# A hybrid attention block on one Trainium2 core: the 16 meta rows stand last in h, and k, v and u come in pieces of 384, 384 and 272 columns

## The chip, the cores and the metric

The kernel runs on one core of a Trainium2 chip. Its time is the device time of one execution in microseconds (us); the kernel before has a median of 738.9 us over three runs (737.64 to 739.29). The engines are PE (TensorE matmul), ACT (ScalarE), DVE (VectorE), POOL (GpSimd) and SP (SyncE, which issues most DMAs). Each engine takes its own instructions in a fixed order and waits on semaphores for the others.

## The reference: what is computed

A pre-norm decoder block with two parallel token mixers over 16 meta rows and 1024 tokens (L = 1040 positions, D = 1024):

```
h = rmsnorm(concat([meta, x]), norm_g)
u_pool, z_pool, q, k, v, z_attn, f_logit, g_pool, g_attn = split(h @ w_in)
y_pool = causal_multiscale_pool(u_pool, pool_w, pool_scale) * silu(z_pool)
log_f  = log_sigmoid(f_logit + b_forget)
# 8 heads of 64; logit[t, s] = q_t.k_s / 8 + sum of log_f over (s, t], causal
y_attn = forgetting_attention(q, k, v, log_f) * silu(z_attn)
merged = sigmoid(g_pool) * (y_pool @ w_up_pool) + sigmoid(g_attn) * (y_attn @ w_up_attn)
out    = rmsnorm((x + merged @ w_out), final_norm_g)      # the meta rows are dropped
```

Only k, v, u and the forget gates are needed for the meta rows; q, the other gates and the output are needed for the 1024 tokens alone. Everything is float32; a product is made of three matmuls in the chip's float32r format (high part times high part, and the two mixed terms).

## The kernel before, in words

**Layout.** h is kept transposed (128 rows of the model dimension in each of 8 slices, tokens along the columns) as a high part `hh` and a low part `hl`. In a row of 1088 columns the 1040 positions are the last 1040, so the meta rows are columns 48 to 63 of the row and the first token is column 64. Every projection is `g_proj` (L166): 24 matmuls (8 slices; `hh,whi`, then `hl,whi`, then `hh,wlo`) of 128 weight columns against a piece of the positions, into one PSUM bank `pj` (three banks in turn). q, the gates and z take two pieces of 512; k, v and u take three `PIECES` of 400, 384 and 256 (L29).

**Start (to about 57 us).** Nine tiles of 128 positions are loaded (`norm_load`, L179; the first one takes the 16 meta rows and 112 tokens in two DMAs, the ninth holds the last 16 tokens), normalised (`norm_stat`, `norm_scale`) and transposed on PE (`norm_t`). Between them the q, k and v of head pair 0 are projected in four pieces (0 to 256, 256 to 512, 512 to 768, 768 to 1040, the loop at L452). The ninth tile is transposed in the middle of the third v piece.

**Evictions.** `q_piece` (L244) has ACT write the high part and DVE the low part of q; `k_piece` (L266) does so for k, each head of the pair apart; `v_piece` (L276) has ACT copy the piece to `VT`. `v_blocks(p, b0, b1)` (L284) then transposes blocks b0 to b1 of 128 keys of `VT` on PE, one matmul `pj<-ident,vt` (L287) a block, and ACT (L292) and DVE (L293) evict them to `V`, a high and a low part for each of two heads. In `f_v` (L319) of the later head pairs the blocks follow the pieces: after the piece that begins at 400 come blocks 0 to 2, after the one at 784 blocks 3 to 5, and blocks 6 to 8 come as a step of their own. Key block b holds keys 128b to 128b + 127 (block 8 the last 128), so each group of blocks ends before the piece that has just been computed begins.

**Attention (about 85 to 480 us).** 16 units (4 head pairs, 2 heads, 2 halves of the queries). `qk` (L596) makes two matmuls `ps<-qa,ka` and `ps<-ql,ka` a key block (L608, L609; two `ps` banks in turn), ACT and DVE evict them as `S` (L617, L615); `maxes` finds column maxima on DVE; `soft` subtracts them (DVE L648), exponentiates (ACT L649), and splits the result (`ph` on ACT L652, `pl` on DVE L653); `av` (L663) multiplies with `V` into `po` (L669).

**What sets the order.** PE's order is that of the code (`manual_schedule`). The attention's steps are written out, and between them `F.pull(ns)` takes matmuls of the later projections from generators (`Fill`): the q, k and v of the next head pair, then u, z and the gates, matmul by matmul, until the given time is filled. The order on ACT, DVE, POOL and SP is set by a scheduler when the program is built. `whi<-raw` (L149, ACT) and `wlo` (L151, POOL) split the weights of the next projection. After the attention come the pooling branch, the merge and the output projection, almost without a gap on PE.

## Time and profile before

| | |
|---|---|
| median of 3 runs | 738.9 us (737.64 to 739.29) |
| profiled execution | 738.82 us, its span (first to last instruction) 737.1 us, so 1.7 us lie around the span |
| busy share of the span | PE 98%, DVE 72%, ACT 51%, POOL 42% |
| chain that ended last | PE 88%, DVE 3%, ACT 1%, POOL 1% |
| its largest part | PE pj L163 (the projections) 66% |
| PE idle, 57 to 490 us, as the waits name it | 1.6 us |

How to read it: PE is busy from the start to the end, so the time is, nearly, the sum of the spacings of PE's matmuls and of the few places where PE waits. A matmul's listed duration overlaps the next one; the spacing of two starts is what it costs. What the other engines do matters only where PE waits for it.

### The profile page before, as it was taken

To read this page: it belongs to the slowest core of one execution; us is meant where nothing else is said; L and a number is where in the kernel's file an instruction comes from. 1 tells how busy PE (TensorE), PEld (TensorE's weight loads), DVE (VectorE), ACT (ScalarE), POOL (GpSimd) and SP (SyncE) were. 2 spreads that over 40 slices of the span, in tenths; PEclk is the share of its full clock that TensorE was granted. 3 is DMA by queue.
4 is the path that set the end of the run, shared out by engine and by line. 5 is a ranking of instruction groups with operands and counts; after the bars stand their busy time and mean duration, and the time that the engine had idled before them with its cause. 6 is when DMAs were issued, how large, how long until landed. Compare 5 with 4: busy or idle time off the path is not lost.

```text
span 737.1 us, 10620 instructions
## 1 busy us (share of the span) xinstructions
PE 725.2 (98%) x3686; PEld 624.2 (85%) x3686; DVE 531.6 (72%) x991; ACT 375.8 (51%) x736; POOL 305.9 (42%) x362
## 2 busy tenths in 40 slices
PE   8999999999999999999999999999999999999996
PEld 6997999988889898889888888888887888888885
DVE  4753578859769878788798688687288554887775
ACT  6652555356456645556554564462545422626445
POOL 4322145465435547336436374283349011006243
PEclk9999999999999999999999999999999999999999
DMA  9201123321452355411542346227485357672006
GB/s 302 61 6 53 28 77 88 98 80 30 109 158 51 94 106 107 120 50 42 177 99 84 98 135 152 73 79 240 138 234 187 113 189 269 222 262 72 1 1 229
DMA packets 82312, 86.89 MB, mean 118 GB/s; under 512 B 9889, under 2 KB 61089, under 8 KB 82226
## 3 DMA queue, kind: packets, MB, share of 16 engines
q1 hardware_dynamic: 78272, 77.29, 34.0%
q0 software_dynamic: 2112, 4.19, 3.6%
q10 hardware_dynamic: 1874, 4.72, 1.7%
q8 instruction: 29, 0.48, 0.3%
q14 instruction: 25, 0.20, 0.1%
HBM read 67.12 MB, written 27.46 MB: 128 GB/s over the span
## 4 chain that ended last, share of the span: by engine, by line
PE 88%; DVE 3%; ACT 1%; issue 1%; POOL 1%; POOLq 0%; ACTq 0%; DVEq 0%
PE pj L163 66%; PE pj L1025 8%; PE po L669 5%; PE ps L609 3%; PE ps L608 2%; PE pt L1025 2%; PE pj L494 1%; POOL yl L136 1%; PE pj L287 0%; DVE S L648 0%; ACT whi L149 0%; DVE pl L653 0%; DVE pt L639 0%; DVE S L615 0%; DVE mt L629 0%
## 5 line engine op out<-in xcount | busy, mean ns | idle before, releaser
L151 POOL TENSOR_TENSOR wlo<-raw,whi 128x256 fp32r<-128x256 f32 x148 | 123.5, 879 | 187.2 <-ACT whi L149 95.9
L163 PE MATMUL pj<-hh,whi 128*128 128x512 f32 (+5 forms) x768 | 178.9, 361 | 0.7 <-DVE V L293 0.4
L163 PE MATMUL pj<-hl,whi 128*128 128x512 f32 (+5 forms) x768 | 175.8, 358 | 0.0
L163 PE MATMUL pj<-hh,wlo 128*128 128x512 f32 (+5 forms) x768 | 173.7, 356 | 0.0
L163 PEld LDWEIGHTS pj<-hh,whi 128*128 128x128 f32 x768 | 132.4, 190 | 17.5 <-PE pj L287 0.6
L163 PEld LDWEIGHTS pj<-hh,wlo 128*128 128x128 f32 x768 | 132.2, 188 | 17.1
L163 PEld LDWEIGHTS pj<-hl,whi 128*128 128x128 f32 x768 | 132.2, 189 | 16.6
L653 DVE TENSOR_TENSOR pl<-S,ph 128x512 fp32r<-128x512 f32 (+4 forms) x112 | 88.3, 806 | 14.0 <-ACT ph L652 13.5
L661 POOL TENSOR_TENSOR acc<-acc,S 128x272 f32<-128x272 f32 (+4 forms) x80 | 77.1, 963 | 8.9 <-ACT S L649 3.7
L617 ACT ACTIVATE S<-ps,negc 128x400 f32<-128x400 f32 (+2 forms) x96 | 49.1, 514 | 48.1 <-DVE S L615 40.5
L649 ACT ACTIVATE S<-S 128x512 f32<-128x512 f32 (+4 forms) x112 | 49.7, 478 | 33.6 <-DVE S L648 33.4
L624 DVE TENSOR_TENSOR m<-m,S 128x272 f32<-128x272 f32 (+4 forms) x80 | 40.9, 512 | 23.1 <-ACT S L617 21.3
L652 ACT ACTIVATE ph<-S 128x512 fp32r<-128x512 f32 (+4 forms) x112 | 51.7, 479 | 9.4 <-PE po L669 8.6
L149 ACT ACTIVATE whi<-raw 128x1024 fp32r<-128x1024 f32 x37 | 39.1, 1056 | 33.6 <-PE pj L163 26.0
L648 DVE TENSOR_TENSOR S<-S,pt 128x512 f32<-128x512 f32 (+4 forms) x112 | 51.7, 498 | 0.8
L873 DVE TENSOR_TENSOR rl<-pj,rl 128x512 f32<-128x512 f32 x32 | 22.1, 690 | 31.5 <-PE pj L163 31.5
L669 PE MATMUL po<-pl,V 128*128 128x512 f32 (+4 forms) x112 | 37.5, 335 | 0.1
L609 PE MATMUL ps<-ql,ka 128*128 128x512 f32 (+4 forms) x112 | 37.4, 334 | 0.0
L615 DVE SCALAR_TENSOR_TENSOR S<-ps,negc,mask 128x128 f32<-128x128 f32 (+2 forms) x72 | 23.7, 330 | 18.8 <-PE ps L609 17.9
L608 PE MATMUL ps<-qa,ka 128*128 128x512 f32 (+4 forms) x112 | 35.9, 321 | 1.2 <-ACT S L617 1.2
L325 ACT ACTIVATE st<-pj 128x512 f32<-128x512 f32 x40 | 23.7, 593 | 26.1 <-PE pj L163 18.8
L1025 PE MATMUL pj<-opy 128*128 128x512 f32 (+1 forms) x168 | 36.2, 374 | 0.0
(187 smaller groups left out, 1101.2 us busy)
## 6 DMA issues: line engine op xcount, KB each, us to landing
raw<-in_w_in_dram SPq DMA_DIRECT2D x40, 512.0 KB, 4.0
sp_gp<-st SPq DMA_DIRECT2D x16, 256.0 KB, 2.0
td<-in_w_out_dram POOLq DMA_DIRECT2D x4, 1024.0 KB, 10.2
sp_ga<-st SPq DMA_DIRECT2D x16, 256.0 KB, 2.0
rl<-sp_gp SPq DMA_DIRECT2D x8, 512.0 KB, 5.3
rl<-sp_ga SPq DMA_DIRECT2D x8, 512.0 KB, 4.7
W<-td SPq DMA_DIRECT2D x8, 512.0 KB, 5.3
xr<-in_x_dram SPq DMA_DIRECT2D x8, 512.0 KB, 4.2
```

The lines of the kernel that those rows point to most:

```text
L151: ins = nc.gpsimd.tensor_tensor(lo[:, k:k + 2], raw[:, k:k + 2], r32(hi[:, k:k + 2]), op=ALU.subtract)
L163: nc.tensor.matmul(ps, a, b, start=(i == 0), stop=(i == len(seq) - 1))
L608: nc.tensor.matmul(ps[:kb, c0:], ka[:, k0:k0 + kb], qa[:, q0 + c0:q0 + 512], start=True, stop=False)
L609: nc.tensor.matmul(ps[:kb, c0:], ka[:, k0:k0 + kb], ql[:, q0 + c0:q0 + 512], start=False, stop=True)
L617: nc.scalar.activation(s[:kb, f0:], ps[:kb, f0:], AF.Identity, bias=nb_)
L648: nc.vector.tensor_tensor(s[:kb, c0:], s[:kb, c0:], self.pm[:kb, c0:], op=ALU.subtract)
L649: exps.append(nc.scalar.activation(s[:kb, c0:], s[:kb, c0:], AF.Exp))
L652: nc.scalar.activation(ph[:kb, c0:], s[:kb, c0:], AF.Copy)
L653: dves.append(nc.vector.tensor_tensor(pl[:kb, c0:], s[:kb, c0:], r32(ph[:kb, c0:]), op=ALU.subtract))
L661: accs.append(nc.gpsimd.tensor_tensor(acc[:kb, c0:], acc[:kb, c0:], s[:kb, c0:], op=ALU.add))
L669: nc.tensor.matmul(self.po[:, c0:], v, r[:kb, c0:], start=(b == 0 and i == 0), stop=(b == self.nb - 1 and i == 1))
L1025: nc.tensor.matmul(ps, pick(A_, k, p)[:, i * 128:(i + 1) * 128], pick(B_, k, q)[:, c0:c1], start=start and n == 0, stop=n == 11, skip_grou ...
```

## The change

h holds the 1024 tokens as columns 0 to 1023 and the meta rows as columns 1024 to 1039; a row stays 1088 columns long and the positions are now its first 1040. Tile 0 is loaded by one DMA of 128 tokens, and the ninth tile is the 16 meta rows. The pieces of k, v and u are 384, 384 and 272. Keys, values and u still keep the meta rows in front: `keys_of` maps columns of h to key positions (16 further on, and the meta rows to 0), and where a piece runs past column 1024 its evictions are made in two parts, 256 columns and 16. Key block 0 is now complete only with the last piece, so the block groups of `v_blocks` are 1 to 3, 4 to 6, and 7, 8 and 0; the last group is evicted in two parts for each head.

```
-PIECES = ((0, 400), (400, 784), (784, 1040))
+PIECES = ((0, 384), (384, 768), (768, 1040))
...
-    hh4 = [hp.tile([128, 4, HROW], F32R, name=f"hh{j}")[:, :, HROW - L:] for j in range(2)]
+    hh4 = [hp.tile([128, 4, HROW], F32R, name=f"hh{j}")[:, :, :L] for j in range(2)]
...
-        if i == 0:
-            nc.sync.dma_start(xt[NM:], x2[:128 - NM, :])
-            nc.sync.dma_start(xt[:NM], meta)
-        else:
-            nc.sync.dma_start(xt[:n], x2[c0 - NM:c0 - NM + n, :])
+        nc.sync.dma_start(xt[:n], meta if n < 128 else x2[c0:c0 + n, :])
...
+    def keys_of(t0, t1):
+        r = [(0, min(t1, SEQ) - t0, t0 + NM)]
+        if t1 > SEQ:
+            r.append((SEQ - t0, t1 - t0, 0))
+        return [(slice(a, b), slice(d, d + b - a)) for a, b, d in r]
...
-                nc.scalar.activation(KA[p, e][a, t0:t1], ps[a], AF.Copy)
+                for c, d in keys_of(t0, t1):
+                    nc.scalar.activation(KA[p, e][a, d], ps[a, c], AF.Copy)
...
-        nc.scalar.activation(VT[p][:, t0:t1], ps, AF.Copy)
+        for c, d in keys_of(t0, t1):
+            nc.scalar.activation(VT[p][:, d], ps[:, c], AF.Copy)
...
-    def v_blocks(p, b0, b1):
+    def v_blocks(p, *parts):
         pt = pj.tile([128, 4, 2, 64], F32, name="pj")
-        for b in range(b0, b1):
-            nc.tensor.transpose(pt[:, b - b0], VT[p][:, KS[b]:KS[b] + KB], ident)
-            yield 109.0
...
+        for b0, b1 in parts:
+            for b in range(b0, b1):
+                nc.tensor.transpose(pt[:, n], VT[p][:, KS[b]:KS[b] + KB], ident)
...
             if c0:
-                yield from v_blocks(p, c0 // KB - 3, c0 // KB)
+                yield from v_blocks(p, (c0 // KB - 2, c0 // KB + 1))
...
-            stores.append(nc.sync.dma_start(dt[:, c0:c1], st))
+            for c, d in keys_of(c0, c1):
+                last = nc.sync.dma_start(dt[:, d], st[:, c])
+            stores.append(last)
...
-        todo += [("q", t0, t1), ("k", t0, t1), ("v", t0, t1)]
+        todo += [("q", t0, min(t1, SEQ)), ("k", t0, t1), ("v", t0, t1)]
...
-            run(q_piece(0, wq, max(NM, t0), t1))
+            run(q_piece(0, wq, t0, t1))
...
-            run(v_blocks(0, 2 * (n // 3) - 2, 2 * (n // 3)))
+            run(v_blocks(0, (max(1, 2 * (n // 3) - 2), 2 * (n // 3))))
...
-            F.add(f"v{p}", v_blocks(p, 6, 9), 4 * p - 2, apart=True)
+            F.add(f"v{p}", v_blocks(p, (7, 9), (0, 1)), 4 * p - 2, apart=True)
```

**PE, the second and third v piece of head pair 1.** In the order of the kernel before (`pj<-ident,vt` are the block transposes, `hh_120,wlo` the last matmuls of a piece, `[waits ...]` names the engine that a row waits for):

```order
L163 MATMUL pj<-hh_120,wlo 128x384 x4
L287 MATMUL pj<-ident,vt 128x128 [waits Activation_49]
L287 MATMUL pj<-ident,vt 128x128 x2
L163 MATMUL pj<-hh_119,whi 128x256 x4
L163 MATMUL pj<-hh_120,whi 128x256 x4
L163 MATMUL pj<-hl_121,whi 128x256 x4
L163 MATMUL pj<-hl_122,whi 128x256 x4
L163 MATMUL pj<-hh_119,wlo 128x256 x4
L163 MATMUL pj<-hh_120,wlo 128x256 x4
L287 MATMUL pj<-ident,vt 128x128 [waits Activation_49]
L287 MATMUL pj<-ident,vt 128x128 x2
```

And in that of the changed kernel:

```order
L163 MATMUL pj<-hh_120,wlo 128x384 x4
L293 MATMUL pj<-ident,vt 128x128 [waits Activation_49]
L293 MATMUL pj<-ident,vt 128x128
L293 MATMUL pj<-ident,vt 128x128 [waits Activation_49]
L163 MATMUL pj<-hh_119,whi 128x272 x4
L163 MATMUL pj<-hh_120,whi 128x272 x4
L163 MATMUL pj<-hl_121,whi 128x272 x4
L163 MATMUL pj<-hl_122,whi 128x272 x4
L163 MATMUL pj<-hh_119,wlo 128x272 x4
L163 MATMUL pj<-hh_120,wlo 128x272 x4
L293 MATMUL pj<-ident,vt 128x128 x2
L293 MATMUL pj<-ident,vt 128x128 [waits Activation_49]
```

The pieces and the transposes stand where they stood, but the last of each three transposes now has a wait for ACT of its own: block 3 reads key columns of the piece just before it, and so does block 6.

**ACT, the same place.** `vt<-pj` is the eviction of a v piece, `S<-S` the exponentials, `ph<-S` the high parts, `V<-pj` the evictions of the transposed blocks. Before:

```order
L649 ACTIVATE S<-S 128x512 [waits DVE_49]
L652 ACTIVATE ph<-S 128x512 [waits Activation_49]
L278 ACTIVATE vt<-pj 128x384 [waits PE_49]
L292 ACTIVATE V<-pj 128x3x64 [waits PE_49]
L649 ACTIVATE S<-S 128x512 [waits DVE_49] x2
L292 ACTIVATE V<-pj 128x3x64 [waits DVE_49]
L652 ACTIVATE ph<-S 128x512 [waits Activation_49] x2
L649 ACTIVATE S<-S 128x512 [waits DVE_49]
L278 ACTIVATE vt<-pj 128x256 [waits PE_49]
L292 ACTIVATE V<-pj 128x3x64 [waits PE_49]
L149 ACTIVATE whi<-raw 128x1024 [waits DMAHW3_49]
```

And changed:

```order
L662 ACTIVATE S<-S 128x512 [waits DVE_49]
L665 ACTIVATE ph<-S 128x512 [waits Activation_49]
L282 ACTIVATE vt<-pj 128x384 [waits PE_49]
L662 ACTIVATE S<-S 128x512 [waits DVE_49]
L302 ACTIVATE V<-pj 128x3x64 [waits PE_49]
L665 ACTIVATE ph<-S 128x512 [waits Activation_49]
L662 ACTIVATE S<-S 128x512 [waits DVE_49]
L302 ACTIVATE V<-pj 128x3x64 [waits DVE_49]
L665 ACTIVATE ph<-S 128x512 [waits Activation_49]
L662 ACTIVATE S<-S 128x512 [waits DVE_49]
L149 ACTIVATE whi<-raw 128x1024 [waits DMAHW6_49,PE_49]
L282 ACTIVATE vt<-pj 128x256 [waits PE_49]
```

The second 384-column eviction stands behind the same `S` and `ph` rows as before; the one of 256 columns has moved from ahead of the weight split `whi` to behind it.

**ACT, the first unit of the attention (about 85 to 90 us).** `S<-ps` are the evictions of the scores. Before:

```order
L292 ACTIVATE V<-pj 128x3x64 [waits PE_49]
L271 ACTIVATE ka<-pj 64x384 [waits PE_49]
L292 ACTIVATE V<-pj 128x3x64 [waits DVE_49]
L617 ACTIVATE S<-ps,negc 128x400 [waits DVE_49]
L271 ACTIVATE ka<-pj 64x384 [waits DVE_49]
L617 ACTIVATE S<-ps,negc 128x272 [waits DVE_49]
L149 ACTIVATE whi<-raw 128x1024 [waits PE_49,DMAHW5_49,Activation_49,Pool_49]
L617 ACTIVATE S<-ps,negc 128x144 [waits DVE_49]
L617 ACTIVATE S<-ps,negc 128x16 [waits DVE_49]
```

And changed:

```order
L302 ACTIVATE V<-pj 128x3x64 [waits PE_49]
L273 ACTIVATE ka<-pj 64x384 [waits DVE_49]
L302 ACTIVATE V<-pj 128x64 [waits DVE_49]
L630 ACTIVATE S<-ps,negc 128x400 [waits DVE_49]
L302 ACTIVATE V<-pj 128x3x64 [waits DVE_49]
L630 ACTIVATE S<-ps,negc 128x272 [waits DVE_49]
L302 ACTIVATE V<-pj 128x64 [waits DVE_49]
L630 ACTIVATE S<-ps,negc 128x144 [waits DVE_49]
L149 ACTIVATE whi<-raw 128x1024 [waits PE_49,DMAHW4_49,Activation_49,Pool_49]
```

The weight split `whi` has moved from ahead of the 144-column score eviction to behind it, and the two heads' evictions of `V` have two parts each.

## Rows read from the trace of the kernel before

**Rows 1.** The page: busy time, share of the span and instructions of each engine.

```profile
PE 725.2 (98%) x3686; PEld 624.2 (85%) x3686; DVE 531.6 (72%) x991; ACT 375.8 (51%) x736; POOL 305.9 (42%) x362
```

**Rows 2.** Waits of PE: who waited for whom, us in total, times, longest.

```profile
PE ps L608 <- ACT S L617: 1.2, 2, 0.9
```

**Rows 3.** Timeline, v of pair 1: start, length (us), engine, line, tiles, count [idle before].

```profile
169.67 1.55 PE L163 MATMUL pj<-hh,wlo 128*128 128x384 f32 x8
...
171.06 0.49 PE L287 MATMUL pj<-ident,vt 128*128 128x128 f32 x3
...
171.25 0.63 ACT L649 ACTIVATE S<-S 128x512 f32<-128x512 f32 x1 [1.94 <-DVE S L648]
...
172.44 0.47 ACT L278 ACTIVATE vt<-pj 128x384 f32<-128x384 f32 x1
...
173.30 1.12 PE L163 MATMUL pj<-hh,wlo 128*128 128x256 f32 x8
...
174.26 0.49 PE L287 MATMUL pj<-ident,vt 128*128 128x128 f32 x3
...
175.14 0.47 PE L163 MATMUL pj<-hh,whi 128*128 128x512 f32 x1 [0.39 <-DVE V L293]
...
175.84 0.39 ACT L278 ACTIVATE vt<-pj 128x256 f32<-128x256 f32 x1
...
176.31 1.08 ACT L149 ACTIVATE whi<-raw 128x1024 fp32r<-128x1024 f32 x1
```

**Rows 4.** Timeline, v of pair 2.

```profile
269.92 0.51 PE L287 MATMUL pj<-ident,vt 128*128 128x128 f32 x3
269.94 0.49 ACT L278 ACTIVATE vt<-pj 128x384 f32<-128x384 f32 x1 [2.11 <-PE pj L163]
...
273.36 0.49 PE L287 MATMUL pj<-ident,vt 128*128 128x128 f32 x3
...
274.21 0.37 ACT L278 ACTIVATE vt<-pj 128x256 f32<-128x256 f32 x1
```

**Rows 5.** Timeline, v of pair 3.

```profile
367.51 0.27 PE L287 MATMUL pj<-ident,vt 128*128 128x128 f32 x1
...
367.71 0.49 ACT L278 ACTIVATE vt<-pj 128x384 f32<-128x384 f32 x1 [0.91 <-PE pj L163]
...
372.39 0.49 PE L287 MATMUL pj<-ident,vt 128*128 128x128 f32 x3
...
372.59 0.38 ACT L278 ACTIVATE vt<-pj 128x256 f32<-128x256 f32 x1 [0.20 <-PE pj L163]
```

**Rows 6.** Groups by form: line, engine, tiles, form, count | busy us, mean ns.

```profile
L163 PE MATMUL pj<-hl,whi 128*128 128x400 f32 x80 | 17.9, 348 | 0.0
```

**Rows 7.** Timeline, runs of eight equal matmuls of 400 columns (k of pair 1).

```profile
77.46 1.63 PE L163 MATMUL pj<-hl,whi 128*128 128x400 f32 x8
...
78.93 1.63 PE L163 MATMUL pj<-hh,wlo 128*128 128x400 f32 x8
```

**Rows 8.** Timeline, runs of eight equal matmuls of 272 columns (k of pair 0).

```profile
51.40 1.15 PE L163 MATMUL pj<-hl,whi 128*128 128x272 f32 x8
...
52.38 1.15 PE L163 MATMUL pj<-hh,wlo 128*128 128x272 f32 x8
```

**Rows 9.** Timeline, the start: the DMA of the meta rows, the first weight split.

```profile
1.25 0.41 SPq L185 DMA_DIRECT2D xt<-in_meta_tokens_dram  x1
...
9.30 1.06 ACT L409 ACTIVATE whi<-raw 128x1024 fp32r<-128x1024 f32 x1 [0.53 <-DMA raw<-in_w_in_dram]
```

**Rows 10.** Timeline, the fourth q piece of pair 0.

```profile
47.23 1.36 PE L163 MATMUL pj<-hh,whi 128*128 128x272 f32 x8 [0.35 <-ACT hh L209]
```

**Rows 11.** Timeline, the first unit of the attention.

```profile
88.67 1.06 ACT L149 ACTIVATE whi<-raw 128x1024 fp32r<-128x1024 f32 x1 [0.31 <-PE pj L163]
...
90.05 0.28 PE L608 MATMUL ps<-qa,ka 128*128 128x16 f32 x1 [0.92 <-ACT S L617]
```

**Rows 12.** The chain that ended last: start, length (us), engine, line, matmuls.

```profile
501.54 60.86 PE pj L163 x268
```

More of the change, by code (lines that the diff above doesn't have):

```diff
@@ L127, in rstd_of @@
         return r
-    hh4 = [hp.tile([128, 4, HROW], F32R, name=f"hh{j}")[:, :, HROW - L:] for j in range(2)]
-    hl4 = [hp.tile([128, 4, HROW], F32R, name=f"hl{j}")[:, :, HROW - L:] for j in range(2)]
+    hh4 = [hp.tile([128, 4, HROW], F32R, name=f"hh{j}")[:, :, :L] for j in range(2)]
+    hl4 = [hp.tile([128, 4, HROW], F32R, name=f"hl{j}")[:, :, :L] for j in range(2)]
     hh = [hh4[k // 4][:, k % 4, :] for k in range(KO)]
@@ L242, in alloc_k, with q_piece @@
             KA[p, e] = gp.tile([128, L], F32R, name="ka", tag="g")
-    def q_piece(p, w, t0, t1):
-        c0, c1 = t0 - NM, t1 - NM
-        ps = yield from g_proj(w, t0, t1)
+    def keys_of(t0, t1):
[3 more added lines that the diff above has]
+        return [(slice(a, b), slice(d, d + b - a)) for a, b, d in r]
+    def q_piece(p, w, c0, c1):
+        ps = yield from g_proj(w, c0, c1)
         def hi(e, r):
@@ L270, in k_piece @@
                 a, o = rows(e)
-                nc.scalar.activation(KA[p, e][a, t0:t1], ps[a], AF.Copy)
+                for c, d in keys_of(t0, t1):
+                    nc.scalar.activation(KA[p, e][a, d], ps[a, c], AF.Copy)
             for e in group:
                 a, o = rows(e)
-                nc.vector.tensor_tensor(KA[p, e][o, t0:t1], ps[a], r32(KA[p, e][a, t0:t1]), op=ALU.subtract)
+                for c, d in keys_of(t0, t1):
+                    nc.vector.tensor_tensor(KA[p, e][o, d], ps[a, c], r32(KA[p, e][a, d]), op=ALU.subtract)
     def v_piece(p, w, t0, t1):
         ps = yield from g_proj(w, t0, t1)
-        nc.scalar.activation(VT[p][:, t0:t1], ps, AF.Copy)
+        for c, d in keys_of(t0, t1):
+            nc.scalar.activation(VT[p][:, d], ps[:, c], AF.Copy)
     def v_alloc(p):
@@ L282, in v_alloc @@
             V[p, e] = ap_.tile([KB, NB, 2, 64], F32R, name="V", bufs=3)
-    def v_blocks(p, b0, b1):
+    def v_blocks(p, *parts):
         pt = pj.tile([128, 4, 2, 64], F32, name="pj")
-        for b in range(b0, b1):
-            nc.tensor.transpose(pt[:, b - b0], VT[p][:, KS[b]:KS[b] + KB], ident)
-            yield 109.0
-        pv = pt[:, :b1 - b0]
-        for e in range(2):
-            vh = V[p, e][:, b0:b1, e, :]
-            nc.scalar.activation(vh, pv[:, :, e, :], AF.Copy)
-            nc.vector.tensor_tensor(V[p, e][:, b0:b1, 1 - e, :], pv[:, :, e, :], r32(vh), op=ALU.subtract)
+        n = 0
+        for b0, b1 in parts:
+            for b in range(b0, b1):
+                nc.tensor.transpose(pt[:, n], VT[p][:, KS[b]:KS[b] + KB], ident)
+                n += 1
+                yield 109.0
+        for e in range(2):
+            n = 0
+            for b0, b1 in parts:
+                pv = pt[:, n:n + b1 - b0]
+                n += b1 - b0
+                vh = V[p, e][:, b0:b1, e, :]
+                nc.scalar.activation(vh, pv[:, :, e, :], AF.Copy)
+                nc.vector.tensor_tensor(V[p, e][:, b0:b1, 1 - e, :], pv[:, :, e, :], r32(vh), op=ALU.subtract)
     def f_q(p):
@@ L298, in f_q @@
         for c0, c1 in HALVES:
-            yield from q_piece(p, w, NM + c0, NM + c1)
+            yield from q_piece(p, w, c0, c1)
     def f_k(p):
@@ L322, in f_raw @@
         for c0, c1 in HALVES:
-            ps = yield from g_proj(w, NM + c0, NM + c1)
+            ps = yield from g_proj(w, c0, c1)
             st = stg.tile([128, 512], F32, name="st")
@@ L495, in gates @@
                                  start=(i == 0), stop=(i == 2 * KO - 1))
-            nc.vector.tensor_copy(fT[:, t0:t1], ps[:16, :t1 - t0])
+            for c, d in keys_of(t0, t1):
+                nc.vector.tensor_copy(fT[:, d], ps[:16, c])
         F.pull(LATENCY)
@@ L709, in pair_fill @@
             F.add(f"v{p}", f_v(p), 4 * p - 2)
-            F.add(f"v{p}", v_blocks(p, 6, 9), 4 * p - 2, apart=True)
+            F.add(f"v{p}", v_blocks(p, (7, 9), (0, 1)), 4 * p - 2, apart=True)
     pair_fill(1)
     gates()
-    run(v_blocks(0, 6, 9))
+    run(v_blocks(0, (6, 9), (0, 1)))
     units = [Unit(p, e, half) for p in range(4) for e in range(2) for half in range(2)]
@@ L783, in f_za @@
         for c0, c1 in HALVES:
-            ps = yield from g_proj(w, NM + c0, NM + c1)
+            ps = yield from g_proj(w, c0, c1)
             evacs.append(nc.scalar.activation(za[p][:, c0:c1], ps, AF.Silu))
```

## The prediction

> **What bounds the kernel now.** I read the page first. PE is busy for 725.2 of 737.1 us [rows 1], so PE sets the end, and the question is only what its matmuls cost and where it waits. Next came PE's waits: between 57 and 490 us, with the attention and all the fills in it, PE idles 1.6 us in three places: twice a score matmul waits for ACT's eviction, 1.2 us in all [rows 2], and once a projection waits 0.39 us for DVE's eviction of `V` [rows 3]. Third, the timeline at the places where the order of the changed kernel differs: the block transposes of v [rows 3 to 5], the start [rows 9, 10] and the first unit [rows 11]. The reader is to see there, for each instruction of PE, which eviction it needs and how long before that eviction has ended. In the kernel before a group of block transposes starts as soon as a piece of v has been computed, and it needs nothing of that piece.
>
> **What the change does to PE's own work: almost nothing.** A pair's k, v or a u chunk still has 1040 columns and 24 matmuls a piece. The pieces' spacings come from runs of eight: 400 columns, 77.46 to 78.93, 1.47 us or 184 ns each [rows 7]; 384 columns, 169.67 to 171.06, 1.39 us or 174 ns; 256 columns, 173.30 to 174.26, 0.96 us or 120 ns [rows 3]; 272 columns, 51.40 to 52.38, 0.98 us or 122 ns [rows 8]. The last was read outside the fills; from 256 to 384 the fills show 54 ns for 128 columns, so 272 there may be 120 + 7 = 127 ns. Three matmuls, one of each piece, cost 184 + 174 + 120 = 478 ns before and 174 + 174 + 122 to 127 = 470 to 475 ns after. A form has 80 matmuls in each of three operand pairs [rows 6], so there are 240 such triples in the fills: a gain of 0.7 to 1.9 us if the new pieces run as these rows do. I take 0.8, near the lower end, since the 272 is the uncertain one and I keep to the rate of the fills; the bounds are 0 (only columns count) and 3.4 (below, the rival on the other side).
>
> The Trainium skill (TensorE: Matmul & The Clock Gate, Back-to-back issue gap) gives the spacing as the columns at the full clock plus a constant per matmul. By that rule three pieces with 1040 columns in all cost the same however they are cut, and this term is zero, the sum 741.5 in place of 740.7. The spacings here do not lie on one such line: from 384 to 400 columns they rise by 10 ns, twice what the columns between 256 and 384 would give [rows 3, 7].
>
> **The new wait.** It is the largest term. `f_v` now puts blocks 1 to 3 behind the second piece and blocks 4 to 6 behind the third. The second piece fills keys 400 to 783 and block 3 is keys 384 to 511; the third fills 784 to 1039, and block 6 is keys 768 to 895. So the last transpose of each group needs ACT's copy of the piece that PE has finished just before, and in PE's order it now waits for ACT. PE takes its instructions in order, so all that stands behind the transpose (the next piece, the next scores) waits as well. There are two such places in each of three head pairs; pair 0 does it at the start with other groups that need older pieces, and costs nothing. Each place, with 0.11 us for a transpose (0.49 us is listed for three, with overlap; I use the spacing that leads to the next piece) and 0.1 us from ACT's end to PE's start, an estimate:
>
> - Pair 1, second piece. PE would come to block 3 at 171.06 + 0.22 = 171.28. On ACT the copy of 384 columns stands behind one `S` and one `ph`, as before, and `S` waits for DVE, so the copy keeps its place: 172.44 + 0.47 = 172.91 [rows 3]. PE goes on at 173.0: 1.7 us.
> - Pair 1, third piece. From 173.0, one transpose and 24 matmuls of 0.122 and two more transposes, PE comes to block 6 at about 176.35. ACT runs seven instructions (three `S`, two `ph`, two `V`) between the copies before, from 172.91 to 175.84; the same seven stand there now, and then the weight split `whi`, 1.08 us, which stood behind the copy before [rows 3]. So the copy ends at 175.84 + 1.08 + 0.39 = 177.3, PE goes on at 177.4: 1.05 us.
> - Pair 2, second piece. ACT is idle and waits for PE [rows 4], the best case: copy from 269.94 to 270.43. PE comes to block 3 at about 270.1 (two `po` matmuls stand among the transposes now): 0.45 us.
> - Pair 2, third piece. Before, the copy ended 274.58 and the transposes began 273.36 [rows 4]. PE now arrives 0.45 later and two transposes further, at 274.05; ACT's chain ahead of the copy hangs half on PE, so the copy ends between 274.6 and 275.1: 0.7 us.
> - Pair 3, second piece. Copy 367.71 to 368.20; two score matmuls of 400 columns stand among the transposes, so PE arrives at about 368.1 [rows 5]: 0.2 us.
> - Pair 3, third piece. Copy 372.59 to 372.97, both it and PE's arrival (372.61) some 0.2 later [rows 5]: 0.4 us.
>
> Together 4.5 us. From below: if ACT were free at all six, each would cost as the third, at most 0.45, and some less: 2.1 us. From above: one more instruction of 0.63 ahead of each copy, 4.5 + 3.8 = 8.3 us.
>
> **What goes.** (1) The wait of 0.39 at 175.14 for DVE's second `V` [rows 3]: PE gets there two us later, so it is covered: -0.4. (2) At 47.23 PE waits for the ninth tile [rows 10]; the fourth q piece no longer needs that tile, only k after it does, some 2.9 us later. The row gives 0.35 of idle time, and the matmul before it also is spaced 0.1 to 0.2 long: -0.5, and what is late next is the k piece, whose inputs are there. (3) In the first unit PE waits 0.92 us at 90.05 for a score eviction that stands behind a weight split of 1.06 us [rows 11]; the split now stands behind that eviction. Two more evictions of `V` stand ahead of it instead, in a chain in which ACT and DVE wait for each other, each at most as long as the 0.39 of a 256-column copy. I take -0.8; bounds -0.9 and +0.3. (4) At the start the DMA of the meta rows, 0.41 us on SP with 0.05 to the next, goes from ahead of all other loads [rows 9]. ACT's first split waits 0.53 for weights at 9.30, so up to 0.46 may be gained for all that follows. Part of that may be lost again, because the other loads share the DMA engines, so I take -0.3; bounds -0.5 and 0.
>
> **What is added beside other work.** 20 evictions on ACT and 17 on DVE, of 16 to 128 columns, each at most 0.39 us [rows 3], under ACT at 51% and DVE at 72% [rows 1]; four more small DMAs of u, which only the pooling branch reads back. The parts of `V` in the last block group lengthen the chain between ACT and DVE and stand ahead of score evictions: +0.3 for three pairs, bounds 0 and 2.3 (two evictions of 0.39 three times).
>
> **The sum.** 4.5 - 0.4 - 0.5 - 0.8 - 0.3 - 0.8 + 0.3 = +2.0; rounded down to 1.9, since PE's arrival also comes a little later after each wait. The profiled execution took 738.8 us (737.1 and 1.7 around), 0.1 below the median of 738.9: 738.8 + 1.9 = 740.7 us.
>
> **Rivals.**
> - Only the copies' own time is waited for (2.1 us, ACT is ready each time, as in rows 4 and 5), and the gains stand (2.8): 738.8 + 2.1 - 2.8 + 0.3 = 738.4, no change. For it: ACT was idle ahead of three of the six copies. Against it: in pair 1 the copy stood 1.4 us behind the end of its piece.
> - ACT is later still: with what it now has to do ahead of the copies, the six waits reach 8.3 us: 738.8 + 1.9 + 3.8 = 744.5. For it: in pair 1 the third piece's copy now stands behind a split of 1.08 us. Against it: in pairs 2 and 3 ACT's order ahead of the copies is what it was.
> - Only columns count on PE (the constant spacing): the piece term is zero, 741.5.
> - The other side, faster: the new pieces begin at columns 0, 384 and 768 of a row, the old ones at 48, 448 and 832, and if that is what made 400, 384 and 256 slow, the new ones run at the rate of the 512-column matmuls, 60.86 us for 268, 227 ns each [rows 12], 0.443 ns a column: 1040 x 0.443 = 461 ns for a triple, 17 below 478, or 4.1 us over 240; with the waits at 2.1 that is 738.8 + 2.1 - 2.0 + 0.3 - 4.1 = 735.1. It is faster from the point where a triple costs less than 468 ns and the waits less than 3 us. Against it: 384 columns already run at 174 from an even column (448).
> - The transposes don't wait at all. In the order they do; I give it no chance of its own.
>
> **How the numbers follow.** The forecast has 0.45, the small waits 0.25, the later ACT 0.10, columns alone 0.12, the other side 0.08. A measurement of this kernel tells 0.2% (1.5 us: 737.4 to 740.4) from no change. Slower: most of the forecast (0.32, since 740.7 is near the bound), the later ACT and 0.10 of columns alone, together 0.52; within: 0.12 of the forecast, 0.02 of columns alone, 0.22 of the small waits, together 0.36; faster: the other side, 0.03 of the small waits and 0.01 of the forecast, 0.12. The range runs from 737.8 to 744.0: below it lies the other side, above it the last part of the later ACT. The forecast's own range is 739.3 to 742.2.
>
> **What would show it.** In the profile after, PE's waits should name `pj<-ident,vt` behind ACT's `vt`, six times, longest in pair 1 (1.7 and about 1 us), and `ps` behind ACT `S` at 90 us should be gone, as should the wait for `hh` before the fourth q piece; runs of eight matmuls of 384 and 272 columns should last 1.39 and 0.98 to 1.02 us. The first split should come near 8.9 us. The forecast is wrong if the transposes' waits come to under 2.5 us or over 7, or if a new wait of over 1 us stands elsewhere on PE.

## The result, and the profile after

The changed kernel takes 740.4 us (median of 7 runs, 740.2 to 742.5); the kernel before, run beside it, 738.4 us (median of 7, 737.6 to 739.3). The ratio is 1.0031, with a 95% interval of 1.0021 to 1.0041: slower by 1.5 to 3.0 us. The forecast was 740.7.

PE's part of the page and the clock row of the profiled execution (span 739.0 us; the answer to [rows 1]):

```profile
PE 724.8 (98%) x3686; PEld 622.9 (84%) x3686; DVE 526.6 (71%) x1008; ACT 377.9 (51%) x756; POOL 307.1 (42%) x362
...
PEclk9999999999999999999999999999999999999999
```

PE is busy for 0.4 us less than before, in a span that is 1.9 us longer. So what was lost was lost in waits, and not to the clock (the mean granted clock of the span is 0.998, and 0.999 before). PE's waits (who waited for whom, us in total, times, longest), which answer to [rows 2]:

```profile
PE pj L293 <- ACT vt L282: 3.1, 5, 1.6
...
PE pj L163 <- POOL yl L136: 0.5, 1, 0.5
PE ps L621 <- ACT S L630: 0.5, 1, 0.5
```

The first line is new, and its name is the one the prediction gave. The wait for `yl` is in the kernel before too (0.6 us). The two waits of `ps` for `S` have become one, in another place. The timeline of PE at v of pair 1, to be laid beside [rows 3]:

```profile
171.57 0.33 PE L293 MATMUL pj<-ident,vt 128*128 128x128 f32 x1 [1.55 <-ACT vt L282]
171.66 1.24 PE L163 MATMUL pj<-hh,whi 128*128 128x272 f32 x8
172.74 1.17 PE L163 MATMUL pj<-hl,whi 128*128 128x272 f32 x8
173.74 1.17 PE L163 MATMUL pj<-hh,wlo 128*128 128x272 f32 x8
174.75 0.38 PE L293 MATMUL pj<-ident,vt 128*128 128x128 f32 x2
175.84 0.33 PE L293 MATMUL pj<-ident,vt 128*128 128x128 f32 x1 [0.72 <-ACT vt L282]
175.94 0.47 PE L163 MATMUL pj<-hh,whi 128*128 128x512 f32 x1
```

And ACT in the same stretch:

```profile
170.51 0.63 ACT L665 ACTIVATE ph<-S 128x512 fp32r<-128x512 f32 x1
171.04 0.47 ACT L282 ACTIVATE vt<-pj 128x384 f32<-128x384 f32 x1
...
174.46 1.05 ACT L149 ACTIVATE whi<-raw 128x1024 fp32r<-128x1024 f32 x1
175.41 0.46 ACT L282 ACTIVATE vt<-pj 128x256 f32<-128x256 f32 x2
```

Two transposes go at once, and the third stands until the copy of 384 columns has ended at 171.51; the second group's last stands until the copy behind the weight split has ended. The wait for DVE's `V` in front of the next piece (0.39 us in [rows 3]) is gone. Pairs 2 and 3, beside [rows 4, 5] (the third of these rows shows no idle time, because the listed durations of the score matmuls before it reach up to it; laid beside the trace before, it comes 0.15 us later than the transpose ahead of it would have it):

```profile
271.33 0.33 PE L293 MATMUL pj<-ident,vt 128*128 128x128 f32 x1 [0.16 <-ACT vt L282]
...
275.57 0.33 PE L293 MATMUL pj<-ident,vt 128*128 128x128 f32 x1 [0.44 <-ACT vt L282]
```

```profile
369.17 0.33 PE L293 MATMUL pj<-ident,vt 128*128 128x128 f32 x1
...
374.30 0.33 PE L293 MATMUL pj<-ident,vt 128*128 128x128 f32 x1 [0.26 <-ACT vt L282]
```

The start, the fourth q piece and the first unit, beside [rows 9 to 11]:

```profile
8.22 1.06 ACT L421 ACTIVATE whi<-raw 128x1024 fp32r<-128x1024 f32 x1 [1.34 <-DMA raw<-in_w_in_dram]
...
46.70 1.12 PE L163 MATMUL pj<-hh,whi 128*128 128x256 f32 x8
...
88.06 1.05 ACT L149 ACTIVATE whi<-raw 128x1024 fp32r<-128x1024 f32 x1
...
88.21 0.28 PE L621 MATMUL ps<-qa,ka 128*128 128x16 f32 x1
...
101.73 0.50 PE L621 MATMUL ps<-qa,ka 128*128 128x512 f32 x1 [0.51 <-ACT S L630]
```

The split is 1.08 us earlier, the wait ahead of the fourth q piece is gone, and the `ps` that waited 0.92 us no longer waits; 0.51 us came back 13 us later, a wait that the prediction did not have.

**Where the time went.** I laid the two traces side by side: for the same matmul, its start after minus its start before. This difference is -0.3 us at 10.2 and again at 17.7 us, 0.0 at 27, -0.8 at 53, -1.8 at 88 (behind the missing 0.92), -1.3 at 102 (the new 0.51), and -1.4 just ahead of v of pair 1. It jumps to +0.3 at the first waiting transpose and from +0.5 to +1.4 at the second, and falls to +0.8 where the wait for `V` was. Pairs 2 and 3 add jumps of 0.34, 0.61, 0.15 and 0.42; a wait of 0.30 for `S` at 360 us, in the kernel before, is not there after; a new wait for DVE's `pl` at 232 us (+0.3) and one that went at 347 us (-0.25) cancel. PE's last matmul comes 1.6 us later. The last 0.3 of the 1.9 lie behind PE, where the output is written out.

### The profile page after: what moved, and what is told of

The parts are those of the page before. It is cut to its first block, busy times and chain, and to the rows that moved or that the text cites. A ratio compares the mean times of both kernels' runs of the same rounds, so it can differ in the third digit from the quotient of the medians.

```text
span 739.0 us, 10674 instructions
## 1 busy us (share of the span) xinstructions
PE 724.8 (98%) x3686; PEld 622.9 (84%) x3686; DVE 526.6 (71%) x1008; ACT 377.9 (51%) x756; POOL 307.1 (42%) x362
## 4 chain that ended last, share of the span: by engine, by line
PE 88%; DVE 3%; ACT 2%; POOL 1%; issue 1%; POOLq 0%; ACTq 0%
PE pj L163 66%; PE pj L1038 8%; PE po L682 5%; PE ps L622 3%; PE ps L621 2%; PE pt L1038 2%; PE pj L506 1%; POOL yl L136 1%; PE pj L293 0%; DVE S L661 0%; ACT whi L149 0%; DVE pl L666 0%; ACT S L662 0%; ACT ph L665 0%; DVE m L637 0%
## 5 line engine op out<-in xcount | busy, mean ns | idle before, releaser
L163 PE MATMUL pj<-hh,whi 128*128 128x512 f32 (+3 forms) x768 | 177.3, 359 | 0.2 <-ACT hh L216 0.2
L163 PE MATMUL pj<-hl,whi 128*128 128x512 f32 (+3 forms) x768 | 175.7, 357 | 0.0
L163 PE MATMUL pj<-hh,wlo 128*128 128x512 f32 (+3 forms) x768 | 173.0, 356 | 0.0
L666 DVE TENSOR_TENSOR pl<-S,ph 128x512 fp32r<-128x512 f32 (+4 forms) x112 | 84.9, 773 | 18.9 <-ACT ph L665 17.7
```

Of the source, the lines that this page charges most:

```text
L163: nc.tensor.matmul(ps, a, b, start=(i == 0), stop=(i == len(seq) - 1))
L666: dves.append(nc.vector.tensor_tensor(pl[:kb, c0:], s[:kb, c0:], r32(ph[:kb, c0:]), op=ALU.subtract))
```

## The experiments

Unless said otherwise each is timed against the kernel before, run on the same chip, and the ratio's interval is at 95%.

**Take the transposes one block later.** Edit of the kernel after:

```
-  yield from v_blocks(p, (c0 // KB - 2, c0 // KB + 1))
+  yield from v_blocks(p, (1, 3) if c0 == PIECES[1][0] else (3, 6))
...
-  F.add(f"v{p}", v_blocks(p, (7, 9), (0, 1)), 4 * p - 2, apart=True)
+  F.add(f"v{p}", v_blocks(p, (6, 9), (0, 1)), 4 * p - 2, apart=True)
```

> The kernel after, with the transposes of V's key blocks taken one block later: (1, 3) behind the second v piece, (3, 6) behind the third, (6, 9) and (0, 1) at the end, so that no transpose reads a vt that ACT has just begun to copy. Theory (the loss is TensorE waiting for ACT's vt copies): the pj waits behind vt fall from 3.1 us to below 0.5, the jumps that they bring (4.2 us in all against the kernel before) go, and the time falls by 3.5 to 4.5 us from the kernel after, to about 736.3: 1.5 to 2.5 us faster than the kernel before. Rival (the loss is the extra evictions in two parts and the piece sizes, and the waits are merely where slack shows): the waits go but the time stays within 1 us of the kernel after, 739.5 to 740.5.

Measured: 737.8 us, ratio 0.9985 (0.9971 to 0.9999), 2.6 below the kernel after's median. The wait behind `vt` is gone from the list, and PE stands 1.95 us ahead of the kernel before at 464 us, where the kernel after stood 1.6 behind. 0.4 of this stood already at 27 us, ahead of any edit; 3.1 came between 164 and 464 us, a little below the 3.5 to 4.5 expected, and the time of 736.3 was missed by 1.5. In the profiled execution the lead was then lost within a few matmuls, at a place the change does not touch. Its PE:

```profile
564.29 1.07 PE L163 MATMUL pj<-yh,whu 128*128 128x512 f32 x4
567.88 2.08 PE L163 MATMUL pj<-yl,whu 128*128 128x512 f32 x4 [2.52 <-POOL yl L136]
```

That is the wait of 0.5 us for POOL, now 2.5 us. I come back to it below. The rival (cost in the extra evictions, 739.5 to 740.5) is out.

**Do the same harm to the kernel before.**

```
-  yield from v_blocks(p, c0 // KB - 3, c0 // KB)
+  yield from v_blocks(p, *((0, 4) if c0 == PIECES[1][0] else (4, 7)))
...
-  F.add(f"v{p}", v_blocks(p, 6, 9), 4 * p - 2, apart=True)
+  F.add(f"v{p}", v_blocks(p, 7, 9), 4 * p - 2, apart=True)
```

> The kernel before with one thing changed: blocks (0, 4) behind the second v piece, (4, 7) behind the third, (7, 9) at the end, so that the last block of a group reads keys of the piece just projected, as in the kernel after. Theory: six waits of pj behind ACT's vt, 2.5 to 5 us of lost time in all, 741 to 743. Rival (the waits come from the new piece sizes or from work that the change put ahead of vt on ACT): under 1 us, 738 to 739.

Measured: 743.0 us, ratio 1.0049 (1.0030 to 1.0067), 4.1 us; in the trace +4.3 us at 389 us, of which 0.3 stood already at 27 us, ahead of any edit, and 4.0 came at v of the three pairs. PE at v of pair 1:

```profile
173.30 0.33 PE L287 MATMUL pj<-ident,vt 128*128 128x128 f32 x1 [1.43 <-ACT vt L278]
...
177.67 0.33 PE L287 MATMUL pj<-ident,vt 128*128 128x128 f32 x1 [0.95 <-ACT vt L278]
```

So a transpose that reads the piece just computed costs this whatever the pieces are.

**The evictions in two parts alone.** In the kernel before:

```
+  def keys_of(t0, t1):
+      cut = [t0, t1] if t1 < L else [t0, t1 - NM, t1]
+      return [(slice(a - t0, b - t0), slice(a, b)) for a, b in zip(cut, cut[1:])]
...
-  F.add(f"v{p}", v_blocks(p, 6, 9), 4 * p - 2, apart=True)
+  F.add(f"v{p}", v_blocks(p, (6, 8), (8, 9)), 4 * p - 2, apart=True)
```

with the loops over `keys_of` of the kernel after.

> The kernel before with the evictions in two parts alone: of each last k, v, u and gate piece the last 16 columns are evicted by an instruction of their own (for u stored by a DMA of their own), and V's last group is evicted as two blocks and one. Prediction's theory: these lie beside TensorE's work and cost 0 to 0.6 us, 738.4 to 739. Rival (the many small instructions on ACT and DVE are what the change costs): 1.5 to 2.5 us, about 740.3.

Measured: 739.0 us, ratio 1.0004 (0.9990 to 1.0017); the profiled span is 0.1 us longer. The small instructions cost nothing that can be measured.

**The old pieces in the new order of h.**

```
-  PIECES = ((0, 384), (384, 768), (768, 1040))
+  PIECES = ((0, 400), (400, 784), (784, 1040))
```

> The kernel after with pieces of 400, 384 and 256 columns, as before, the same blocks behind the same pieces. By the spacings in the two traces (three matmuls of 400, 384 and 256 columns 184.6 + 177.2 + 122.4 ns, two of 384 and one of 272 in the kernel after 2 x 176.4 + 129.2 ns, about 240 of each) the sizes are worth 0.3 to 0.6 us and the vt copy of 256 columns ends a little earlier than that of 272: the time stays within 0.7 us of the kernel after, at about 740.6. Rival, the prediction's term (0.8 us or more for the sizes): 741.2 or above. If a piece of 384 columns that starts at a multiple of 128 is better than one of 400 for its place and not its size, the 384 and the 256 here are longer than in the kernel after.

Measured: 741.8 us, ratio 1.0044 (1.0029 to 1.0059), 1.4 above the kernel after's median: the number fits the rival, but not its reason. The matmuls became cheaper, not dearer. Over 67 to 400 us the mean spacing of 400, 384 and 256 columns is 182.5 + 175.7 + 121.1 = 479.3 ns, against 176.5 + 176.5 + 128.9 = 481.9 ns in the kernel after and 184.6 + 177.1 + 122.4 = 484.1 ns before. What was lost is two waits for `S`, one of them the 0.92 us of [rows 11], back because the split stands ahead of the 144-column eviction again. ACT and PE of this kernel:

```profile
87.88 1.06 ACT L149 ACTIVATE whi<-raw 128x1024 fp32r<-128x1024 f32 x1 [0.21 <-PE pj L163]
...
88.95 0.54 ACT L630 ACTIVATE S<-ps,negc 128x144 f32<-128x144 f32 x2
```

```profile
89.37 0.28 PE L621 MATMUL ps<-qa,ka 128*128 128x16 f32 x1 [0.92 <-ACT S L630]
```

That tests the third gain: the same wait, to the hundredth, is back with the place of the split, though the pieces changed with it. The wait of 0.51 us at 101.73 in the kernel after is gone here (the difference rises by 1.00 at the first and falls by 0.55 at the second), so the two trade places, and the net of both is some 0.4 us. The second wait is 0.66 us at 363 us, where the kernel after has none.

**Only the place of h in its row.** The kernel after with h in the last 1040 of 1088 columns:

```
-  ... name=f"hh{j}")[:, :, :L] ...
+  ... name=f"hh{j}")[:, :, HROW - L:] ...
```

(and `hl` in the same way)

> The kernel after with h laid in the last 1040 columns of its rows of 1088, as before, and not in the first: each piece starts 48 columns further into the row, nothing else changes. Theory (the place of a piece in h's row sets the spacing of its matmuls; in the kernel before the 256-column matmuls of the first 60 us are spaced 114 ns at the median with this offset, in the kernel after 120 ns without it): 200 such matmuls go back to about 114 ns, the start gains 0.8 to 1.2 us, and the time is 739.3 to 740. Rival (the spacing comes from what runs beside them in the start, or from the pieces' order): the median stays at 120 ns and the time within 0.4 us of the kernel after, at 740.4.

Measured: 745.8 us, ratio 1.0094 (1.0080 to 1.0109), 5.3 above the kernel after. The expectation held for the 256-column matmuls and missed the rest. By 53 us this kernel is 0.8 us ahead of the kernel after, as the 114 ns would have it; then it loses 6.3 us up to 560 us, spread over the whole stretch, because the 512-column matmuls, which begin at 48 and 560 of the row here, are spaced 233 ns in place of 227. PE at two runs of eight in a stretch without waits, of the kernel after and of this one:

```profile
509.66 1.98 PE L163 MATMUL pj<-hl,whi 128*128 128x512 f32 x8
511.47 1.75 PE L163 MATMUL pj<-hh,wlo 128*128 128x512 f32 x7
```

```profile
508.19 2.03 PE L163 MATMUL pj<-hl,whi 128*128 128x512 f32 x8
510.06 2.03 PE L163 MATMUL pj<-hh,wlo 128*128 128x512 f32 x8
```

1.81 us a run against 1.87. And at the 256-column pieces of the start, again the kernel after and this one:

```profile
34.53 1.12 PE L163 MATMUL pj<-hh,whi 128*128 128x256 f32 x8
35.49 1.12 PE L163 MATMUL pj<-hl,whi 128*128 128x256 f32 x8
```

```profile
33.98 1.07 PE L163 MATMUL pj<-hh,whi 128*128 128x256 f32 x8
34.89 1.07 PE L163 MATMUL pj<-hl,whi 128*128 128x256 f32 x8
```

0.96 against 0.91 us. There are about 1300 matmuls of 512 columns from h; their mean rises by 4.0 ns in the fills and by 6.7 in the 245 or so of 505 to 566 us: 4.2 + 1.6 = 5.8 us, nearly all of the loss.

**The fourth k piece first.**

```
+  todo[9:11] = [todo[10], todo[9]]
   for n, (kind, t0, t1) in enumerate(todo):
```

> The kernel after with the fourth k piece of the start taken ahead of the fourth q piece, so that the piece that reads the ninth tile comes first again, as the q piece did before. Prediction's theory (0.5 us gained because the first of the fourth pieces no longer waits for the ninth tile): TensorE waits 0.3 to 0.6 us behind ACT's hh at about 47 us, and this stays to the end: 740.8 to 741. Rival (what the start loses is made up by the gates' waits): no difference of the place of the gates' first matmul, 740.4.

Measured: 741.7 us, ratio 1.0042 (1.0029 to 1.0054). PE's first matmul of the fourth pieces waits again, nearly as in [rows 10]:

```profile
47.20 1.37 PE L163 MATMUL pj<-hh,whi 128*128 128x272 f32 x8 [0.32 <-ACT hh L205]
```

The difference to the kernel after jumps by 0.69 us here and keeps that size to 568 us, where this execution too met the 2.5 us wait for POOL. The gain of 0.5 to 0.7 us is shown in the trace. The medians lie 1.3 us apart, more than expected; how many of the runs met that wait, no trace shows.

**Older blocks, and V stored in their order.**

```
-          for b0, b1 in parts:
-              pv = pt[:, n:n + b1 - b0]
-              n += b1 - b0
-              vh = V[p, e][:, b0:b1, e, :]
+          s0 = (parts[0][0] - 1) % NB
+          n = sum(b1 - b0 for b0, b1 in parts)
+          pv = pt[:, :n]
+          vh = V[p, e][:, s0:s0 + n, e, :]
...
-          v = V[self.p, self.e][:kb, b].rearrange("p j d -> p (j d)")
+          v = V[self.p, self.e][:kb, (b - 1) % NB].rearrange("p j d -> p (j d)")
```

> The kernel with the transposes of V's blocks taken one block later (1, 3 then 3, 6 then 6, 7, 8, 0), and V's blocks stored in that order (block 0 as the last of nine), so that each group is evicted whole: two fewer ACT and two fewer DVE instructions for each pair. Theory (V's parts lie beside TensorE's work): no waits behind vt, and within 0.5 us of the same without the new order of V, 737.4 to 737.9. Rival (ACT and DVE are short of time in the first units): 0.5 to 1.5 us less, 736.3 to 737.2.

Measured: 736.8 us (736.6 to 737.2, 6 runs), ratio 0.9973 (0.9962 to 0.9984): faster than both kernels, by 2.0 us than the one before. The median lies in the rival's range, but mostly not for its reason. At 464 us this kernel stands at -1.98 us and the one with older blocks at -1.95, of which that one had 0.27 more than this one at 57 us already. So behind the start this kernel gains 0.3 more, at 293 us, where a wait of 0.15 us for ACT's `S` is not there: the fewer evictions are worth at most that, below the rival's 0.5. The rest is the tail, where this execution has no wait of PE for `yl`. At v of pair 1 the three transposes run through, and a short wait for `V` is back:

```profile
172.83 0.49 PE L293 MATMUL pj<-ident,vt 128*128 128x128 f32 x3
173.56 0.70 PE L163 MATMUL pj<-hh,whi 128*128 128x512 f32 x2 [0.24 <-DVE V L302]
```

**The meta rows loaded early, a failed try.**

```
+  spare = ap_.tile([NM, D], F32, name="spare", tag="t")
+  xts = {0: norm_load(0)}
+  nc.sync.dma_start(spare, meta)
+  xts[1] = norm_load(1)
```

> The kernel after with the 16 meta rows loaded a second time, into a tile that nothing reads, between the loads of the first and the second tile on SP's queue, where the kernel before had them. Prediction's term: the first weight split moves back from 8.2 to about 9 us and the start loses 0.3 us, 740.7. Rival (the first transposes begin at 8.01 us in either kernel, and what follows is set elsewhere): the place of the transposes of the second tile and all behind it moves by less than 0.1 us, 740.4.

Measured: 744.7 us, ratio 1.0086 (1.0071 to 1.0102). It answers another question: the tile's buffer was the one that holds `norm_g`, so SP waited for its reader, and all loads behind it came late:

```profile
SPq L404 <- PE gb L414: 4.0, 1, 4.0
```

A delay of 3.8 us at 11 us is still 3.8 at 568 and 3.9 at the end: the start is worth its full time.

**The meta rows early, in a buffer of their own.**

```
+  spare = ap_.tile([KB, 512], F32, name="spare", tag="acc", bufs=2)
+  xts = {0: norm_load(0)}
+  nc.sync.dma_start(spare[:32], meta.rearrange("m (b c) -> (m b) c", b=2))
+  xts[1] = norm_load(1)
```

> The kernel after with the 16 meta rows loaded a second time, into a tile that nothing reads and nothing else has used, between the loads of the first and second tile on SP's queue; the load waits for nothing. Prediction's term: first weight split back from 8.2 to about 9 us, the start 0.3 us longer, 740.7. Rival (what follows is set elsewhere): all from 27 us on within 0.1 us of the kernel after, 740.4.

Measured: 740.9 us, ratio 1.0034 (1.0021 to 1.0047). The first split is back where it was, and the fourth tile's transposes start at 21.14 in place of 20.36 us. ACT and PE:

```profile
9.28 1.06 ACT L424 ACTIVATE whi<-raw 128x1024 fp32r<-128x1024 f32 x1 [0.55 <-DMA raw<-in_w_in_dram]
```

```profile
21.14 1.04 PE L214 MATMUL pt<-ident,xt 128*128 128x128 f32 x8
```

The +0.77 us stays to 568 us, where the 0.5 us wait for POOL falls away and takes most of it back. But not all of it comes from the load. The transposes of the second tile and a run of eight of the first q piece behind them, in the kernel before, the kernel after and this one:

```profile
10.49 1.09 PE L218 MATMUL pn<-ident,xt 128*128 128x128 f32 x4 [0.51 <-PE pt L218]
...
14.51 1.46 PE L163 MATMUL pj<-hl,whi 128*128 128x240 f32 x8
```

```profile
10.20 1.09 PE L214 MATMUL pn<-ident,xt 128*128 128x128 f32 x4 [0.22 <-PE pt L214]
...
13.78 1.12 PE L163 MATMUL pj<-hl,whi 128*128 128x256 f32 x8
```

```profile
10.45 1.09 PE L214 MATMUL pn<-ident,xt 128*128 128x128 f32 x4 [0.47 <-PE pt L214]
...
14.48 1.91 PE L163 MATMUL pj<-hl,whi 128*128 128x256 f32 x8
```

Up to the first q piece the load costs 0.25 us, and without it the change gained 0.29: near the prediction's 0.3. The other 0.5 us arise in that piece, whose matmuls are spaced 213 ns up to 16.6 us here, but 120 ns from 12.5 us on, with a short wait at 13 us, in the kernel after. This is not the load either: the kernel of the last experiment below has no such load, and has the wide spacing up to 16.1 us.

**Other places of h.** The kernel with older blocks and V in their order, with h shifted by 32 columns (`[:, :, 32:32 + L]`), and the kernel before with h at the start of its rows (`[:, :, :L]`):

> The kernel with older blocks and V stored in their order, with h shifted by 32 columns in its rows. In the kernel after (pieces of 512 columns at 0 and 512 of the row) these matmuls are spaced 227 ns at the median, shifted by 48 columns 233 ns; those of 256 columns in the start 120 ns and shifted by 48 columns 114 ns. Theory (anything but a multiple of 64 columns slows the 512-column matmuls by about 6 ns, some 1000 of them): 232 to 233 ns, 741.5 to 742.5. Rival (the step is only for odd multiples of 16 columns): 227 ns, and with 114 ns in the start 736 to 736.8.

> The kernel before with h laid in the first 1040 columns of its rows: every piece starts 48 columns earlier in the row (512-column pieces at 16 and 528, the pieces of 400, 384 and 256 at 0, 400 and 784), nothing else changes. Theory (the place of a piece in h's row sets its spacing): the 512-column matmuls, at multiples of 64 columns before, go from 227 to 230 to 233 ns and the time to 741 to 744; the 400-column ones at 0 go from 184 to 180 ns, the 256-column ones of the start from 114 to 118 to 120. Rival (the place does not matter in the kernel before): 738.4 to 739.

Measured: 742.2 us, ratio 1.0051 (1.0037 to 1.0066), and 739.6 us, ratio 1.0013 (1.0004 to 1.0022). Spacings of 512 columns: 232 ns where the pieces begin 32 columns past a multiple of 64, and 229 to 230 ns at 16 past (the kernel before has them at 64 and 576, 227 ns). The theory held for the 512-column pieces; for the second kernel the time came out below the expected range: in the fills the mean of the 512-column matmuls rose by only 0.9 ns (1 us in all), and the pieces gained 1.3 us, since a triple went from 484 to 479 ns (400 columns from 184 to 180 ns at column 0).

**Using it in the start.** The kernel with older blocks and V in their order, with

```
-  for t0, t1 in ((0, 256), (256, 512), (512, 768), (768, L)):
+  for t0, t1 in ((0, 240), (240, 496), (496, 752), (752, L)):
```

> The kernel with older blocks and V stored in their order, and in the start pieces that end at columns 240, 496 and 752 instead of 256, 512 and 768, so that the 256-column pieces begin at 240 and 496, which are 48 columns past a multiple of 64, as such pieces began in the kernel before; everything behind the start is as it was. Theory (the place of a piece in h's row sets its spacing): the 256-column matmuls of the start go from 120 to 114 ns at the median, the gates begin 0.5 to 1 us earlier, and the time is 735.8 to 736.4. Rival (the two bounds of 16 columns more in the last piece and the tiles' waits eat it): the gates begin within 0.3 us, 736.8.

Measured: 737.2 us, ratio 0.9973 (0.9958 to 0.9989): no gain. The 256-column matmuls run at 114 ns, as the theory has it, but the gates begin 0.4 us later. The first tiles' work comes 0.8 us later at 17 us and has made that up at 31 to 37 us; the last pieces, of 288 columns, lose 0.4 again. The first piece is late because its matmuls are spaced 213 ns up to 16.1 us, where the kernel that it is compared with has 120 ns from 12.3 us on, with a short wait at 13 us.

## Why the prediction was right, point by point

- **The new wait: right in kind, place and size.** Predicted for the six places 1.7, 1.05, 0.45, 0.7, 0.2 and 0.4, together 4.5 us. Read off the two traces' difference at the transposes: 1.72, 0.88, 0.34, 0.61, 0.15 and 0.42, together 4.1. Taking the transposes one block later gives 3.1 (older blocks) and 3.5 us (with V in their order) back between 164 and 464 us; 4.1 less the 0.6 that the wait had covered is 3.5. Doing the same harm to the kernel before costs 4.0 to 4.1. The rival of small waits (2.1) fell in pair 1, where the copy stood behind other work on ACT; in the second pieces of pairs 2 and 3, where ACT was ready, the waits were as small as it said.
- **(1) DVE's V in the cover of the wait**: predicted -0.4; the difference falls by 0.57 where that wait was.
- **(2) The fourth q piece**: predicted -0.5; -0.6 in the trace (another 0.1 is the 16 columns that this piece has fewer), 0.69 when undone.
- **(3) The split behind the score eviction**: predicted -0.8; -1.0 in the trace, back in the kernel with the old pieces together with the split's place. Not foreseen: a new wait for `S` of 0.51 us at 101.73, which went when the first came back, so that half of the gain was lost again; and 0.30 us at 360 that went. Why these two moved was not tested.
- **(4) The start: right in size, and then used up by a term that was missed.** Predicted -0.3, bounds -0.5 and 0. PE stands 0.29 us ahead at the second tile's transposes and 0.30 at 17.7 us, and loading the meta rows early costs 0.25 of it. The split itself moved further, by 1.08 us to 8.22 and not to 8.9, but PE's next work moved by the 0.29 alone. At 27 us nothing is left of it, since the 256-column matmuls of the start went from 114 to 120 ns, up to 0.06 us in each run of eight. Shifting h back by 48 columns returned 0.8 us by 53 us. The prediction counted columns there and looked at the place only for the fills.
- **The pieces**: predicted -0.8; 484.1 to 481.9 ns a triple is -0.5 over 240. The reason given (400 columns are dear for their size) was wrong: with the pieces of before laid at 0, 400 and 784 a triple is 479.3, the cheapest of the three. It also rested on a slip: 10 ns from 384 to 400 columns is one and a half times, not twice, what the columns between 256 and 384 would give (54 ns for 128 columns, 6.8 for 16). What made 400 columns dear was in part their place. So the rival on the other side had the right cause in it (the old pieces began at 48) with a price that was too high: 400 columns gained 2 to 4 ns from it, not 7. (The upper bound of 3.4 us that the prediction takes from this rival is not the 4.1 us that the rival gives.)
- **The added evictions**: predicted +0.3; 0.0004 of the time alone, with an interval that spans zero, and at most 0.3 us when V's parts were joined.

The sum by these: 4.1 - 0.6 - 0.6 - 1.0 + 0.5 - 0.3 - 0.5 = +1.6, with nothing for the start and the evictions. It is what PE's last matmul shows; the spans differ by 1.9 and the medians by 2.1. That the forecast of 1.9 came out nearly to the point is in part luck: the terms that came out lower (waits, gains 1 to 3, evictions, the wait at 360) make 1.5 us, those that came out higher (start, pieces, the new wait for `S`) 1.1, and the two nearly cancelled.

The rule weighed in the prediction (the Trainium skill, TensorE: Matmul & The Clock Gate, Back-to-back issue gap: columns at the full clock and a constant, which the page gives for a single matmul by itself) does not hold in this stream of weight loads and matmuls. The same 512 columns with the same weights are spaced 227, 230, 232 or 233 ns by where they begin in a row.

## What to carry to other kernels

A small edit of indices can set one engine to read what another has only just begun to copy: for each such read, ask how far behind the copy stands in its engine's queue, and keep the reader one unit of work behind its producer; that was worth more than 3 us here, more than everything else in the change. When an operand's place in its row moves, look at the spacing of every size that reads it, since one size can gain what another loses. A kernel that wins in the middle may still hand its lead to a wait near the end: compare the place of the same instruction at several points before believing the total. And look at the spacing of the first matmuls before putting a difference of the start down to an edit.

## What the runs showed that I had not expected

**The place of the moving operand.** Spacing at the median by where the piece begins, in columns past a multiple of 64 of h's row:

```
columns     +0         +16    +32    +48
512         227 ns     230    232    233
256         120        117    120    114
```

The 256 columns at +16 are those of one piece of the fills (at 784; 118 ns in the kernel with the old pieces); the same size at +0 in the fills (at 832) has 120. The cause is not known; what the columns are next to in the other operands was not varied.

**The first piece runs at two rates.** In most traces the first q piece begins at a spacing of 213 ns and goes on at about 112 to 120 ns, nearly the two spacings' ratio that the next paragraph has with the granted clock beside it. The change comes at 15.3 us in the kernel before, 12.4 after, 16.7 with the meta rows early and 16.2 in the last experiment; with older blocks the whole piece has the narrow spacing. PE had been at work since 1.3 us in all of them, with idle stretches of 0.1 to 0.5 us from 7 us on. Kernels with the same start differ here, so it is not an edit's doing. Up to 0.5 us of difference at 27 us between two profiled executions (0.4 with older blocks, 0.3 and 0.5 in the two edits of the kernel before) comes ahead of any edit, and is not counted as an effect above.

**A short pause that can halve the clock.** The kernel with older blocks, in stretches of time (from and to in us, length, each engine's busy time; the last three figures are the granted clock as a share of full speed, the DMA share and GB/s):

```profile
core 0: us, PE busy (x) PEld busy (x) DVE busy (x) ACT busy (x) POOL busy (x), PEclk, DMA share, GB/s
...
564.00:568.00 4.00, 1.48 (x8) 0.90 (x6) 2.70 (x2) 3.76 (x5) 4.00 (x5) 0.96 1.06 414
568.00:571.00 3.00, 3.00 (x7) 2.36 (x8) 0.00 (x0) 1.35 (x2) 1.21 (x2) 0.50 0.95 270
571.00:580.00 9.00, 9.00 (x41) 7.40 (x40) 7.43 (x9) 4.65 (x6) 0.00 (x0) 1.00 0.38 139
```

Behind 2.52 us of waiting the clock is granted at 0.50 for three microseconds, 1.2 GHz of 2.4, and six matmuls are spaced 427 ns in place of 227: with the first one, another 1.5 us. The kernel with the old pieces shows the same; in the one with k first the wait is 2.54 us and the granted clock behind it 1.00, so such a wait does not always have this sequel. The wait has its start 15 us earlier: DVE waits 0.36 us for a DMA that brings `rc`, and POOL's last subtractions begin 1.0 us late relative to PE. As I read it, the later they are, the more of them run beside DVE's two-input products, where one takes 1.7 us in place of 0.7. POOL's subtractions in this kernel (ns min/median/max):

```profile
L136 POOL TENSOR_TENSOR yl<-rl,yh x16: 724/1640/1737, 541.5 to 568.5; 128x256 fp32r<-128x256 f32 x16
```

Of the fourteen traces three have a wait for `rc` of 0.36 to 0.43 us there (older blocks, old pieces, k first), and these three alone have the 2.5 us: POOL's last subtractions begin 2.1 us ahead of PE's first matmul of `yh` in them. In the traces with 0.5 to 0.65 us of waiting, the kernels before and after among them, they begin 3.0 to 3.2 us ahead, and 3.2 to 3.5 in those with none. Why the DMA came late was not tested. The Trainium skill (SBUF — State Buffer, SBUF: two separate sides) says that DVE, in an operation with two SBUF inputs, and GpSimd hold a shared port in turn, a whole instruction at a time; the two durations agree with that. Medians of kernels that meet this wait in different shares can differ by some tenths of a microsecond for no reason of their own.
